# Mixer of a two-layer hybrid block: index keys first, index scores in two halves of the heads, four output tiles split among the last heads

## The chip, the cores and the metric

The kernel runs on one core of a Trainium2 chip. The metric is the device time of one execution in microseconds (us); the number quoted for the kernel before is the median of three runs. The engines are called TensorE (PE), VectorE (DVE), ScalarE (ACT), GpSimd (POOL) and SyncE (SP), as in the profile.

## The reference, cut to what matters

The program computes two hybrid layers (each: a feed-forward block, a mixer, a second feed-forward block), a norm, and then a second block of four other branches with a feed-forward block of its own. Everything is in 32-bit floats, for one sequence of 512 tokens of width 1024. The change lies in the mixer of the hybrid layers, which runs twice, once in each layer:

```python
h = rmsnorm(x, mix_norm) @ w_in
(a_q, a_k, a_v, b_q, b_k, b_v, i_q, i_k, i_w, c_q, c_kv, c_kr) = split_columns(h)
o_a = chunk_relpos_attention(a_q, a_k, a_v, a_rel_bias)          # 6 heads, additive relative bias
o_b = dsa_attention(rope(b_q), rope(b_k), b_v,                   # 5 heads, only the best 128 keys of a query
                    rope(i_q), rope(i_k), i_w)                   # 8 index heads of 32 choose them
o_c = mla_attention(c_q, c_kv, c_kr, ...)                        # 5 heads from two latents
x = x + jnp.concatenate([o_a, o_b, o_c], axis=-1) @ w_out
```

Inside `dsa_attention` the index heads give one score for each query and key, the sum over the eight heads of a weight times `relu(q_idx . k_idx)`; keys of later chunks get a large negative number, and the best 128 of each query are kept:

```python
dots = jnp.einsum('bqhd,bsd->bqhs', qi, k_idx) * (IDX_DIM ** -0.5)
score = jnp.einsum('bqh,bqhs->bqs', wi, jax.nn.relu(dots))
score = jnp.where(adm[None], score, NEG)
_, idx = lax.top_k(score, topk)
```

## The kernel before

Activations lie with features on the 128 partitions and the 512 tokens along the free axis. A matrix product in 32-bit precision is made of three TensorE passes over operands that are split into a high and a low part: `mm3` (L311 to L315) issues them, so that L313, L314 and L315 are the three passes of every such product. The split of an activation is one copy on ACT (L307) and one subtraction on DVE (L308, `split`); a weight is loaded on SP (L294), its high part is copied on ACT or POOL (L298) and its low part is a subtraction on DVE or POOL (L301).

The mixer is the method `mix(l)` from L593. It first projects the index queries (two tiles, `qi`) and then the tile that holds the index keys, the index weights and the rotary key of the C heads (tile 2: L619 to L634, with two small SP transfers at L620 and L621 and the split `ki` at the end). A rotary tile (`rope`, L561) scales the projection on DVE (L565), moves blocks of partitions with SP transfers into a tile `g`, multiplies on POOL (L570, L571) and adds on DVE (L572). The step `scores(i)` (L638) makes, for one block i of 128 queries, eight small products of index queries and keys, one for each index head, a ReLU on ACT (L648) and an accumulation on DVE (L650, L652), and then overwrites the inadmissible corner (`memset`). The generator `topk` (L655) then finds the best keys in 16 rounds for each of three blocks, each round a maximum of eight (L660) and a replacement (L661) on DVE; `some(n)` runs n of those 48 rounds.

The remaining steps are latents (L), values (V), the dense projections of A, B and C heads (a, b, c) and the heads themselves (A, B, C). A head computes logits on TensorE (L461 for A and B heads, `mm3` for C heads), adds the bias and takes the row maximum on DVE (L478), exponentiates on ACT (L483), inverts the sum on DVE (L484), scales on POOL (L485), transposes on TensorE (L517), copies and splits the transposed weights on ACT and DVE (L307, L308, tiles `pt`), multiplies with the values on TensorE (L526) and writes the output with a DVE addition (L535) into a tile of the `ys` slots. An A head first loads its bias with SP (L719) and POOL overwrites a corner of it (L720).

The string `MIX_PLAN` gives the order in which the program calls these steps. After the plan, all eight output tiles are split into `hs` slots (L771 to L777), and the output projection runs over them in the order 0, 1, 2, 6, 7, 3, 4, 5: for the first three of its eight column tiles seven of the eight inputs come first (`part`), so that they can be issued ahead of the last heads' end.

The instructions of each engine are not issued in the plan's order but in one that the framework's tile scheduler makes at build time from the plan and its own estimates. A shift in the plan can therefore move instructions of all engines in the whole mixer. Each engine takes its own list strictly in order: an instruction that waits holds back all that stand behind it on that engine.

```python
MIX_PLAN = ("S1 S2 S3 V0 a0 A0 A1 L0 a1 A2 L1 a2 V2 A3 t14 A4 A5 t4 c0 C0 c1 c2 t14 c3 V1 C1 C2 b0 t6 C3 t10 c4 t2 C4 t48 "
            "B0 B1 b1 B2 B3 b2 B4")
```

Of the kernel before, what the change touches and what calls it, by code (L numbers as in the profile page):

```python
# [10 lines left out]
def _warn_once_fixed(msg, *args, **kwargs):  # L11
# [12 lines left out]
S = 512  # L24
D = 1024
KD = 8
# [2 lines left out]
HALVES = ((0, 12), (12, 22))  # L29
DEPTH = 2  # L30
WENG = ("av", "ap")
MIX_PLAN = ("S1 S2 S3 V0 a0 A0 A1 L0 a1 A2 L1 a2 V2 A3 t14 A4 A5 t4 c0 C0 c1 c2 t14 c3 V1 C1 C2 b0 t6 C3 t10 c4 t2 C4 t48 "
            "B0 B1 b1 B2 B3 b2 B4")
FOX_PLAN = ("F0 Q0 K0 V0 Q1 H0 K1 H1 Q2 H2 K2 H3 V1 Q3 H4 K3 H5 Q4 H6 K4 H7 V2 Q5 H8 K5 H9 G0 Q6 H10 K6 G1 H11 V3 Q7 "
            "H12 G2 K7 H13 G3 H14 G4 H15 G5")
SB_PLAN = ("Q0 K0 V0 Q1 K1 H0 G0 H1 Q2 K2 H2 G1 H3 V1 Q3 K3 H4 H5 Q4 K4 H6 G2 H7 V2 Q5 K5 H8 H9 Q6 K6 H10 G3 H11 V3 Q7 K7 "
# [1 line left out]
NEG = -1e30  # L38
# [3 lines left out]
YAT = ((0, 0), (0, 1), (1, 0), (3, 0), (3, 1), (1, 1), (2, 0), (2, 1))  # L42
# [155 lines left out]
class Build:  # L198
# [394 lines left out]
    def mix(self, l):  # L593
        nc, I = self.nc, self.I
        hs, rb, rc = self.norm(f"mix_{l}", spill=True)
        ci, si, tk = (self.table(k) for k in (2, 3, 4))
        win = I[f"win_{l}"]

        def tile_of(n):
            w = self.weights(win[n], D)  # L600
            ps = self.ps()
            self.proj(ps, w, hs)
            return ps

        yslots = {}
# [7 lines left out]
            return yslots[a][64 * s:64 * s + 64, b, :]  # L613


        qi = [self.rope(tile_of(n), rb, 1.0, (ci, si), 16, tag="pt") for n in range(2)]
        ps = tile_of(2)
        f, g, kr = self.f(), self.f("g"), self.mx()
        nc.vector.tensor_mul(f, ps, rb)  # L619
# [8 lines left out]
        nc.tensor.matmul(pk, self.cst[:64, P:2 * P], f[:64], start=True, stop=True)  # L628
        ki = self.hl("pt")
        self.split(ki, pk)  # L630
        nc.gpsimd.tensor_mul(g[96:128], g[96:128], tk[96:128])
        nc.scalar.activation(g[64:96], g[96:128], AF.Copy)
        nc.gpsimd.tensor_add(kr[64:96], f[64:96], g[64:96])
# [1 line left out]

        sel = [None] + [self.mx() for _ in range(3)]

        def scores(i):  # L638
            n = (i + 1) * P
            t = slice(i * P, (i + 1) * P)  # L640
            sc = sel[i][:, :n]
            for h in range(8):
                r = slice(32 * (h % 4), 32 * (h % 4) + 32)
                q = qi[h // 4]
                ps = self.logits()
                self.mm3(ps[:, :n], q[r, 0, t], q[r, 1, t], ki[r, 0, :n], ki[r, 1, :n], True, True)
                e = self.f("fa")
                nc.scalar.activation(e[:, :n], ps[:, :n], AF.Relu)  # L648
                if h:
                    nc.vector.scalar_tensor_tensor(sc, e[:, :n], iw[:, 8 * i + h:8 * i + h + 1], sc, op0=OP.mult, op1=OP.add)  # L650
                else:
                    nc.vector.tensor_scalar(sc, e[:, :n], iw[:, 8 * i + h:8 * i + h + 1], None, op0=OP.mult)  # L652
            nc.vector.memset(sc[0:64, n - 64:n], NEG)

        def topk():  # L655
            for i in range(1, 4):
# [107 lines left out]
        def head_b(h):  # L764
            p, s = divmod(h, 2)
            self.head(*qk["b", p], None,
                      lambda i: sel[i][:, :(i + 1) * P] if i else self.chm[:, S - P:], vb[p], s, yout(6 + h))

        steps = {"S": scores, "L": lambda n: (latent_q, latent_kv)[n](), "V": lambda n: (values_a, values_b, values_c)[n](),
                 "a": dense_a, "A": head_a, "b": dense_b, "B": head_b, "c": dense_c, "C": head_c, "t": some}  # L770
        self.run(MIX_PLAN, steps)  # L771

        ys = [self.hl("hs") for _ in range(KD)]
        order = (0, 1, 2, 6, 7, 3, 4, 5)
        for k in order:
            a, b = YAT[k]
            self.split(ys[k], yslots[a][:, b, :])  # L777
        po = {}
        w = {}

# [566 lines left out]
```

## Time and profile before

| | us |
|---|---|
| median of three runs (lowest, highest) | 3539.57 (3539.09, 3543.49) |
| the profiled execution, its own time | 3545.66 |
| its span in the trace | 3543.9 |
| TensorE busy in the span | 3449.9 (97%) |
| VectorE busy | 1985.0 (56%) |
| GpSimd busy | 1485.8 (42%) |
| ScalarE busy | 1434.4 (40%) |

The first mixer lies at about 380 to 664 us of the span and the second at about 1420 to 1700 us; both run the same list of instructions with other buffers. The granted clock is TensorE's, as a share of its full 2.4 GHz; its other level is 1.2 GHz. A matmul's duration in the trace overlaps the next one's start, so what counts in a row of matmuls is the distance from start to start.

### The profile page before, as it was taken

The page shows a single profiled execution, that of the slowest core. Times are in us where ns is not written, and L with a number is a line of the kernel's source. Part 1 is how long each engine was busy: PE and PEld are TensorE (multiplying, and loading weights), DVE is VectorE, ACT ScalarE, POOL GpSimd, SP SyncE. Part 2 cuts the span into 40 slices and gives each one's busy share as a digit, 9 for nine tenths or more (in the row PEclk, how much of TensorE's full clock was granted, in tenths as well). Part 3 has the DMA queues.
Part 4 walks back from the last instruction along what each step waited for, and adds up shares of the span by engine and source line. Part 5 has one row for each costly group of instructions (what it writes and reads, how often), then busy time and mean ns, then how long its engine had stood idle before and what let it go on. Part 6 is the DMA issues. An engine that isn't in the chain of part 4 may idle for free.

```text
span 3543.9 us, 44752 instructions
## 1 busy us (share of the span) xinstructions
PE 3449.9 (97%) x16392; PEld 2866.2 (81%) x16392; DVE 1985.0 (56%) x3274; ACT 1434.4 (40%) x2366; POOL 1485.8 (42%) x1098
## 2 busy tenths in 40 slices
PE   8999999999999999999999999999999999999999
PEld 7888777788888888777888887888877788888887
DVE  5434697653445345796643456347636657757363
ACT  4223455532233223455422245346635545533222
POOL 3333346342424242446333443248645655435342
PEclk9999999999999999999999999999999999999999
DMA  3333433322333334334323233245532454442332
GB/s 134 91 105 107 130 94 108 114 98 92 101 94 101 90 101 129 104 96 118 113 94 109 84 125 113 96 129 143 154 123 93 147 178 128 128 143 95 96 101 90
DMA packets 141259, 397.57 MB, mean 112 GB/s; under 512 B 18144, under 2 KB 21600, under 8 KB 141040
## 3 DMA queue, kind: packets, MB, share of 16 engines
q1 hardware_dynamic: 141040, 394.71, 36.2%
q8 instruction: 130, 2.13, 0.2%
q14 instruction: 89, 0.73, 0.1%
HBM read 327.24 MB, written 20.48 MB: 98 GB/s over the span
## 4 chain that ended last, share of the span: by engine, by line
PE 48%; DVE 5%; ACT 2%; issue 1%; DMA 1%; POOL 1%; SPq 1%; DVEq 0%; ACTq 0%; POOLq 0%
PE pd L313 10%; PE pd L315 10%; PE pd L314 10%; PE pa L313 4%; PE pa L314 4%; PE pa L315 4%; PE po L526 1%; PE pt L517 1%; DVE wl L301 1%; PE pa L461 1%; ACT wh L298 1%; DVE st L1086 0%; DVE st L478 0%; SPq L454 0%; ACT st L483 0%
## 5 line engine op out<-in xcount | busy, mean ns | idle before, releaser
L301 POOL TENSOR_TENSOR wl<-raw,wh 128x1024 fp32r<-128x1024 f32 (+3 forms) x315 | 717.0, 2276 | 1158.2 <-ACT wh L298 1149.3
L298 ACT ACTIVATE wh<-raw 128x1024 fp32r<-128x1024 f32 (+3 forms) x631 | 609.6, 967 | 1336.6 <-PE pd L314 851.0
L313 PE MATMUL pd<-hs,wh 128*128 128x512 f32 (+1 forms) x2008 | 794.1, 396 | 21.0 <-ACT wh L298 7.7
L315 PE MATMUL pd<-hs,wl 128*128 128x512 f32 (+1 forms) x2008 | 792.7, 395 | 2.9 <-DVE wl L301 1.7
L314 PE MATMUL pd<-hs,wh 128*128 128x512 f32 (+1 forms) x2008 | 791.3, 394 | 1.1 <-DVE hs L308 1.0
L301 DVE TENSOR_TENSOR wl<-raw,wh 128x1024 fp32r<-128x1024 f32 (+3 forms) x316 | 384.0, 1215 | 230.6 <-ACT wh L298 224.0
L313 PEld LDWEIGHTS pd<-hs,wh 128*128 128x128 f32 (+1 forms) x2008 | 379.0, 189 | 102.6 <-ACT wh L298 14.0
L315 PEld LDWEIGHTS pd<-hs,wl 128*128 128x128 f32 (+1 forms) x2008 | 379.2, 189 | 86.6 <-DVE wl L301 4.6
L314 PEld LDWEIGHTS pd<-hs,wh 128*128 128x128 f32 (+1 forms) x2008 | 379.8, 189 | 81.7 <-DVE hs L308 2.7
L313 PE MATMUL pa<-hs,wh 128*128 128x512 f32 x896 | 349.6, 390 | 0.0
L314 PE MATMUL pa<-hs,wh 128*128 128x512 f32 x896 | 349.2, 390 | 0.0
L315 PE MATMUL pa<-hs,wl 128*128 128x512 f32 x896 | 349.2, 390 | 0.0
L413 POOL TENSOR_TENSOR f<-f,g 128x512 f32<-128x512 f32 x88 | 145.8, 1659 | 280.2 <-ACT g L411 273.8
L412 DVE TENSOR_TENSOR f<-pa,rb 128x512 f32<-128x512 f32 x88 | 60.8, 690 | 272.4 <-PE pa L315 272.4
L314 PEld LDWEIGHTS pa<-hs,wh 128*128 128x128 f32 x896 | 168.4, 188 | 35.0
L313 PEld LDWEIGHTS pa<-hs,wh 128*128 128x128 f32 x896 | 168.4, 188 | 34.7
L315 PEld LDWEIGHTS pa<-hs,wl 128*128 128x128 f32 x896 | 168.2, 188 | 34.9
L485 POOL TENSOR_SCALAR st<-st,ta 128x128 f32<-128x128 f32 x192 | 109.3, 573 | 94.2 <-DVE ta L484 81.7
L313 PE MATMUL pd<-ys,wh 128*128 128x512 f32 x362 | 143.9, 398 | 1.8 <-DVE f L740 1.7
L314 PE MATMUL pd<-ys,wh 128*128 128x512 f32 x362 | 142.6, 394 | 0.0
L315 PE MATMUL pd<-ys,wl 128*128 128x512 f32 x362 | 142.6, 394 | 0.0
L308 DVE TENSOR_TENSOR pt<-pt 128x384 fp32r<-128x384 f32 (+1 forms) x200 | 115.9, 595 | 32.7 <-ACT pt L307 31.7
(387 smaller groups left out, 6410.6 us busy)
## 6 DMA issues: line engine op xcount, KB each, us to landing
raw<-in_wg_dram SPq DMA_DIRECT2D x88, 512.0 KB, 3.4
raw<-in_wu_dram SPq DMA_DIRECT2D x88, 512.0 KB, 3.4
raw<-in_win_dram SPq DMA_DIRECT2D x38, 512.0 KB, 3.5
qk<-nt SPq DMA_DIRECT2D x76, 256.0 KB, 3.9
raw<-in_w2gt_dram SPq DMA_DIRECT2D x32, 512.0 KB, 3.4
raw<-in_w2br_dram SPq DMA_DIRECT2D x32, 512.0 KB, 3.3
qk<-nt SPq DMA_DIRECT2D x108, 128.0 KB, 2.5
raw<-in_wd1a_dram SPq DMA_DIRECT2D x32, 384.0 KB, 3.1
```

The lines of the kernel that those rows point to most:

```text
L298: nc.scalar.activation(h[:, :n], raw[:, :n], AF.Copy)
L301: (nc.vector if sub == "v" else nc.gpsimd).tensor_sub(lo[:, :n], raw[:, :n], h[:, :n].bitcast(FT))
L308: (eng or nc.vector).tensor_sub(dst[rows, 1, cols], src, dst[rows, 0, cols].bitcast(FT))
L313: mm(out, wh, xh, start=start, stop=False)
L314: mm(out, wh, xl, start=False, stop=False)
L315: mm(out, wl, xh, start=False, stop=stop)
L412: nc.vector.tensor_mul(u, pu, rb)
L413: nc.gpsimd.tensor_mul(ga, ga, s)
L461: self.nc.tensor.matmul(ps[:, :n], q[:, s, t], k[s][:, x, :n], start=x == 0, stop=x == 1)
L485: nc.gpsimd.tensor_scalar(st[:, c], st[:, c], sm, 0.0, op0=OP.mult, op1=OP.add)
L517: nc.tensor.transpose(pt[:, at + (i - j) * P:at + (i - j + 1) * P], st[:, OFF[i] + j * P:OFF[i] + (j + 1) * P], self.ident)
L526: nc.tensor.matmul(po[:, j * P:], va[:, o:o + P], w[:, x, c:c + S - j * P], start=j == 0 and x == 0, stop=j == 3 and x == 1)
```

## The change

Three edits of `mix`, in the order in which they stand. First, tile 2 (index keys, index weights, rotary key) is projected and treated ahead of the two `qi` tiles. Second, the scores are no longer made block by block with eight heads, but in two halves: `S0` makes heads 0 to 3 for all three blocks and `S1` heads 4 to 7, and only the second half overwrites the corner. The first half needs the first `qi` tile alone. Third, a new step Y splits output tiles 0, 1, 2 and 6 among the last B heads, into `ys` slots, which the latents have left by then; the other four are split after the plan, in `hs` slots, as before. The order of the output projection stays. No operation is added or taken away, and TensorE has 16392 matmuls in both.

```diff
-MIX_PLAN = ("S1 S2 S3 V0 a0 A0 A1 L0 a1 A2 L1 a2 V2 A3 t14 A4 A5 t4 c0 C0 c1 c2 t14 c3 V1 C1 C2 b0 t6 C3 t10 c4 t2 C4 t48 "
-            "B0 B1 b1 B2 B3 b2 B4")
+MIX_PLAN = ("S0 S1 V0 a0 A0 A1 L0 a1 A2 L1 a2 V2 A3 t14 A4 A5 t4 c0 C0 c1 c2 t14 c3 V1 C1 C2 b0 t6 C3 t10 c4 t2 C4 t48 "
+            "B0 Y0 B1 b1 Y1 B2 Y2 B3 b2 Y6 B4")
...
-        qi = [self.rope(tile_of(n), rb, 1.0, (ci, si), 16, tag="pt") for n in range(2)]
         ps = tile_of(2)
...
         self.split(ki, pk)
+        qi = [self.rope(tile_of(n), rb, 1.0, (ci, si), 16, tag="pt") for n in range(2)]
...
-        def scores(i):
+        def scores(a):
+            for i in range(1, 4):
+                four(i, a)
+
+        def four(i, a):
...
-            for h in range(8):
+            for h in range(4 * a, 4 * a + 4):
...
-            nc.vector.memset(sc[0:64, n - 64:n], NEG)
+            if a:
+                nc.vector.memset(sc[0:64, n - 64:n], NEG)
...
+        ys = {}
+
+        def early(k):
+
+            a, b = YAT[k]
+            ys[k] = self.hl("ys")
+            self.split(ys[k], yslots[a][:, b, :])
...
-        ys = [self.hl("hs") for _ in range(KD)]
         order = (0, 1, 2, 6, 7, 3, 4, 5)
         for k in order:
-            a, b = YAT[k]
-            self.split(ys[k], yslots[a][:, b, :])
+            if k not in ys:
+                a, b = YAT[k]
+                ys[k] = self.hl("hs")
+                self.split(ys[k], yslots[a][:, b, :])
```

Lines behind the edits move by 1 to 14 (L660 becomes L665, L661 becomes L666, L733 becomes L738). What the scheduler makes of it is seen in the lists of instructions.

The first place is on TensorE, in the first mixer, where the last C head ends and the B heads begin. Here pd_5457 is the last input projection of this stretch, pd_5611 and pd_5639 are the first two column tiles of the output projection with four inputs each (12 matmuls each), pm_5024 are the last logits of C4, pa_5070 and pa_5079 the first logits of B0. Before:

```order
L315 MATMUL pd_5457<-hs_2570,wl_5453 128x512
L313 MATMUL pd_5611<-hs_5581,wh_5606 128x512
...
L315 MATMUL pd_5611<-hs_5587,wl_5607 128x512
L313 MATMUL pm_5024<-qk_4961,qk_4988 128x512
...
L461 MATMUL pa_5070<-qk_4818,qk_4769 128x128 x2
L313 MATMUL pd_5639<-hs_5581,wh_5634 128x512
...
L315 MATMUL pd_5639<-hs_5587,wl_5635 128x512
L461 MATMUL pa_5079<-qk_4818,qk_4769 128x256 x2
```

Now (pd_5466 is the projection that was pd_5457, pa_5524 are the first logits of B4):

```order
L315 MATMUL pd_5466<-hs_2570,wl_5462 128x512
L313 MATMUL pm_5024<-qk_4961,qk_4988 128x512
...
L461 MATMUL pa_5070<-qk_4818,qk_4769 128x128 x2
L461 MATMUL pa_5079<-qk_4818,qk_4769 128x256 x2
...
L461 MATMUL pa_5524<-qk_5516,qk_5502 128x128 x2
L313 MATMUL pd_5611<-ys_5139,wh_5606 128x512
L313 MATMUL pd_5639<-ys_5139,wh_5634 128x512
```

The 24 matmuls of the output projection that stood around the first logits of B0 now stand some 45 rows later, behind the first logits of B4 and beside the products of B1 and B2.

The second place is on DVE at the same point of the program: hs_5581 to hs_5587 are the four split output tiles, st_4992 the softmax of C4, f_5290 a rotary tile of the B heads. Before:

```order
L308 TENSOR_TENSOR pt_4908<-pt_4904,pt_4908 128x384
L308 TENSOR_TENSOR hs_5581<-ys_3195,hs_5581 128x512
L308 TENSOR_TENSOR hs_5582<-ys_3195,hs_5582 128x512
L308 TENSOR_TENSOR hs_5583<-ys_3997,hs_5583 128x512
L308 TENSOR_TENSOR hs_5587<-ys_4570,hs_5587 128x512
L478 ISA st_4992,ta_4998<-pm_4994,chm_116 128x128
```

Now, at that place, and at the place to which the four have gone (pt_5194 and pt_5203 are transposed weights of B1):

```order
L308 TENSOR_TENSOR pt_4908<-pt_4904,pt_4908 128x384
L478 ISA st_4992,ta_4998<-pm_4994,chm_116 128x128
...
L308 TENSOR_TENSOR pt_5194<-pt_5190,pt_5194 128x384
L308 TENSOR_TENSOR ys_5139<-ys_3195,ys_5139 128x512
L308 TENSOR_TENSOR ys_5312<-ys_3195,ys_5312 128x512
L308 TENSOR_TENSOR ys_5386<-ys_3997,ys_5386 128x512
L308 TENSOR_TENSOR ys_5519<-ys_4570,ys_5519 128x512
L308 TENSOR_TENSOR pt_5203<-pt_5199,pt_5203 128x384
```

The four subtractions no longer stand ahead of C4's softmax; they stand among the softmaxes of B1 to B3.

The third place is on DVE in the middle of the first mixer, where head A3's softmax (st_3881) waits for its bias x_3878; x_2784 is the third block of the top-k. Before:

```order
L660 MAX t8_4924<-x_2784 128x8
L545 SCALAR_TENSOR_TENSOR e_3824<-pd_3826,rc_3719,e_3824 128x2x64
L545 SCALAR_TENSOR_TENSOR e_3824<-pd_3839,rc_3719,e_3824 128x2x64
L661 MATCH_REPLACE x_2784<-t8_4924,x_2784 128x512
L535 TENSOR_TENSOR ys_3195<-po_3566,fa_3633 64x512
L545 SCALAR_TENSOR_TENSOR e_3825<-pd_3826,rc_3719,e_3825 128x64
L545 SCALAR_TENSOR_TENSOR e_3825<-pd_3839,rc_3719,e_3825 128x64
L660 MAX t8_4927<-x_2784 128x8
L478 ISA st_3881,ta_3886<-pa_3883,x_3878 128x128
```

Now:

```order
L665 MAX t8_4840<-x_2784 128x8
L545 SCALAR_TENSOR_TENSOR e_3824<-pd_3839,rc_3719,e_3824 128x2x64
L666 MATCH_REPLACE x_2784<-t8_4840,x_2784 128x512
L545 SCALAR_TENSOR_TENSOR e_3825<-pd_3839,rc_3719,e_3825 128x64
L665 MAX t8_4918<-x_2784 128x8
L545 SCALAR_TENSOR_TENSOR v_3823<-pd_3852,rc_3719,v_3823 128x2x64
L478 ISA st_3881,ta_3886<-pa_3883,x_3878 128x128
```

The round that stands just ahead of st_3881 was the tenth of the third block (its second half, the replacement, follows behind); now it is the seventh, so three rounds more come behind that softmax. The lists of the second mixer move in the same way at the first two places.

## Rows read from the trace of the kernel before

**Rows 1.** Stages of the first mixer: window, length, busy us (instructions), granted clock, DMA

```profile
core 0: us, PE busy (x) PEld busy (x) DVE busy (x) ACT busy (x) POOL busy (x), PEclk, DMA share, GB/s
400.00:500.00 100.00, 100.00 (x489) 78.76 (x488) 91.34 (x234) 51.64 (x101) 44.02 (x39) 0.98 0.40 114
500.00:512.00 12.00, 8.71 (x44) 7.19 (x43) 10.02 (x30) 4.73 (x12) 2.29 (x3) 0.86 0.58 149
512.00:540.00 28.00, 23.41 (x102) 17.80 (x102) 27.03 (x73) 20.20 (x51) 15.61 (x19) 0.87 0.34 103
540.00:600.00 60.00, 59.44 (x336) 52.30 (x335) 39.77 (x102) 35.41 (x81) 34.66 (x34) 0.98 0.32 93
...
622.50:633.00 10.50, 7.04 (x43) 5.50 (x42) 6.95 (x23) 6.46 (x17) 7.69 (x10) 1.00 0.76 183
633.00:654.00 21.00, 19.79 (x110) 15.59 (x110) 16.66 (x56) 16.19 (x44) 9.53 (x17) 1.00 0.12 27
```

**Rows 2.** Waits of PE, 360 to 720 us: line, released by; us in total, times, longest

```profile
PE pa L461 <- DVE ta L478: 6.1, 7, 3.5
...
PE pd L313 <- DVE f L740: 1.7, 2, 1.4
```

**Rows 3.** PE timeline, start of the mixer: start, us, instruction [idle before, releaser]

```profile
387.55 0.50 PE L313 MATMUL pd<-hs,wh 128*128 128x512 f32 x1 [1.53 <-DVE f L565]
...
396.54 0.41 PE L624 MATMUL pa<-cst,f 8*128 8x8 f32 x4
```

**Rows 4.** Timelines of SP and DVE, the bias of head A3

```profile
502.92 3.06 SPq L454 DMA_DIRECT2D qk<-nt  x4
...
511.61 0.29 DVE L478 CUSTOM_DVE_ANT_0 st<-pa,x 128x128 f32<-128x128 f32 x1 [1.99 <-POOL x L720]
```

**Rows 5.** DVE groups by shape, 380 to 600 us: busy us, mean ns | idle before

```profile
L660 DVE MAX8 t<-x 128x8 f32<-128x512 f32 x16 | 10.8, 677 | 0.0
L661 DVE MATCH_REPLACE8 x<-t,x 128x512 f32<-128x512 f32 x16 | 10.8, 674 | 0.0
```

**Rows 6.** PE timeline, end of C4 and start of the B heads

```profile
608.90 0.39 PE L313 MATMUL pd<-hs,wh 128*128 128x512 f32 x1
609.13 0.39 PE L314 MATMUL pd<-hs,wh 128*128 128x512 f32 x1
...
612.38 0.39 PE L313 MATMUL pm<-qk 96*128 96x512 f32 x1
...
616.75 0.69 PE L461 MATMUL pa<-qk 128*128 128x128 f32 x2 [3.50 <-DVE ta L478]
618.17 0.77 PE L313 MATMUL pd<-hs,wh 128*128 128x512 f32 x1 [0.73 <-DVE f L565]
...
619.58 0.63 PE L313 MATMUL pd<-hs,wh 128*128 128x512 f32 x1
620.01 0.63 PE L314 MATMUL pd<-hs,wh 128*128 128x512 f32 x1
...
622.47 0.40 PE L461 MATMUL pa<-qk 128*128 128x256 f32 x2
```

**Rows 7.** DVE timeline, the same stretch

```profile
606.29 5.47 DVE L308 TENSOR_TENSOR hs<-ys,hs 128x512 fp32r<-128x512 f32 x4
...
612.94 2.82 DVE L572 TENSOR_TENSOR f<-f,g 128x512 f32<-128x512 f32 x1 [0.97 <-POOL g L571]
...
618.24 0.56 DVE L478 CUSTOM_DVE_ANT_0 st<-pa,chm 128x384 f32<-128x384 f32 x1
```

**Rows 8.** POOL timeline, the same stretch

```profile
609.60 1.60 POOL L570 TENSOR_TENSOR f<-f,x 128x512 f32<-128x512 f32 x1 [1.30 <-DMA g<-f]
...
612.87 2.34 POOL L301 TENSOR_TENSOR wl<-raw,wh 128x1024 fp32r<-128x1024 f32 x1
```

**Rows 9.** Durations, ns min/median/max: DVE splits of tile hs, 600 to 665 us; POOL L485, 600 to 664 us

```profile
L308 DVE TENSOR_TENSOR hs<-ys,hs x8: 679/692/2572, 606.3 to 661.8; 128x512 fp32r<-128x512 f32 x8
...
L485 POOL TENSOR_SCALAR st<-st,ta x24: 362/532/1213, 618.3 to 651.9; 128x128 f32<-128x128 f32 x6, 128x256 f32<-128x256 f32 x6, 128x384 f32<-128x384 f32 x6, 128x512 f32<-128x512 f32 x6
```

More of the change, by code (lines that the diff above doesn't have):

```diff
@@ L767, in head_b @@
                       lambda i: sel[i][:, :(i + 1) * P] if i else self.chm[:, S - P:], vb[p], s, yout(6 + h))
-        steps = {"S": scores, "L": lambda n: (latent_q, latent_kv)[n](), "V": lambda n: (values_a, values_b, values_c)[n](),
+        ys = {}
[3 more added lines that the diff above has]
+            self.split(ys[k], yslots[a][:, b, :])
+        steps = {"Y": early, "S": scores, "L": lambda n: (latent_q, latent_kv)[n](), "V": lambda n: (values_a, values_b, values_c)[n](),
                  "a": dense_a, "A": head_a, "b": dense_b, "B": head_b, "c": dense_c, "C": head_c, "t": some}
         self.run(MIX_PLAN, steps)
-        ys = [self.hl("hs") for _ in range(KD)]
         order = (0, 1, 2, 6, 7, 3, 4, 5)
         for k in order:
-            a, b = YAT[k]
-            self.split(ys[k], yslots[a][:, b, :])
+            if k not in ys:
+                a, b = YAT[k]
+                ys[k] = self.hl("hs")
+                self.split(ys[k], yslots[a][:, b, :])
         po = {}
```

## The prediction

> **What bounds the kernel now.** The busy shares come first: TensorE is busy 97% of the span, so what any edit of order can win is TensorE's idle time and its time at the lower clock, in the stretches that the edit touches. Next comes the view by stages of the first mixer [rows 1]. From 400 to 500 us TensorE has no idle time at all, with DVE busy 91.34 of 100. From 500 to 512 it is idle 12 - 8.71 = 3.29 us and from 512 to 540 us 28 - 23.41 = 4.59 us, at a granted clock of 0.86 and 0.87; DVE is busy 27.03 of the 28, so the latter stretch is DVE's. From 540 to 600 us TensorE is again full, with DVE at 39.77 of 60. Then come the B heads, where the idle time lies in single waits [rows 6]. The waits of TensorE over the mixer [rows 2] name DVE's softmax (6.1 us over seven waits, on L461 alone) before anything else. The second mixer runs the same list, so all terms are for one mixer and are doubled at the end.
>
> **Start: keys first.** Tile 2 moves ahead of the two query tiles. The wait of 1.53 us [rows 3] belongs to the row scale and stays: the third projection of the group waits for it, whichever tile that is. What is new is that the four small transposes of the index weights (0.41 us, [rows 3]) stand ahead of the third projection and wait for DVE's first product, which the projection needs anyway for its buffer. SP issues the two key transfers ahead of the sixteen of the query tiles instead of behind them. So the index scores can begin some microseconds earlier, and DVE begins its scores earlier too; TensorE has nothing to win from that up to 500 us, as it is never idle there. Price: between 0 and 0.8 us (the transposes, and as much waiting); I take **+0.4 us**, the row's own duration.
>
> **Middle: scores in halves, and where the top-k rounds land.** The head start is worth something only if DVE is further on at 512 us. Head A3's softmax stands in DVE's list behind a bias that SP fetches after the four stacking transfers of a key tile (502.92 us); DVE had run dry for 1.99 us when it came at 511.61 [rows 4]. The changed list leaves this chain as it is, so the 3.29 us from 500 to 512 us stay. And by that point in its list DVE has done three rounds fewer of the third block than before. A round costs 0.677 + 0.674 = 1.35 us [rows 5], so 3 x 1.35 = 4.05 us of DVE work move behind the bias, into the stretch in which DVE is the bound. In exchange, the products that release TensorE's projections (the key products of the C heads, L733 and L740) stand several microseconds of DVE work earlier. The waits for L740 make 1.7 us in two waits [rows 2]. Bounds: all 4.59 us of idle time go, or all 4.05 us of deferred rounds are waited for. I take **-1.7 us**, those two waits alone, because they are the ones whose releaser moves forward, while 20 us of free DVE time from 540 to 600 us [rows 1] can take the rounds.
>
> **End: four splits and 24 matmuls of the output projection move.** Before, the four splits take 5.47 us of DVE at 606.29 us, ahead of C4's softmax [rows 7], and the 24 matmuls that they release fill TensorE: twelve from 608.90 to 612.38 us, at a distance of 0.23 us, and twelve from 618.17 to 622.47 us, most of them 0.43 us apart, which is the 1.2 GHz level, after a wait of 3.50 us [rows 6]. In the changed list nothing stands between C4's last logits and B0's first two, and the 24 come behind B4's first logits.
>
> The wait for B0's first logits hardly moves. DVE's rotary addition at 612.94 us, which stands ahead of the softmax that releases them, waits for POOL, and POOL waited for a transfer until 609.60 us [rows 7, 8]; no split is in that chain. So TensorE now waits from about 609.6 us (608.90 and 0.7 us of logits) to about 616 us, where it waited 3.50 us before. B0's second logits then no longer stand behind twelve slow matmuls: they can start when the reduction of 618.24 us is through, at 618.80 [rows 7], instead of 622.47. That is a lead of 3.7 us for the whole chain of B heads. The 24 matmuls have to be paid later: 24 x 0.23 = 5.5 us, in the stretch that was 633 to 654 us, where TensorE had 21 - 19.79 = 1.2 us of idle time [rows 1]. Sum: 5.5 - 1.2 - 3.7 = **+0.6 us**. The lower bound: they also fill the 10.5 - 7.04 = 3.5 us of idle time from 622.5 to 633 us [rows 1], and DVE's addition shrinks from 2.82 us to a split's 0.69 [rows 7, 9], another 2.1: -5.0 us. The upper: they fill nothing, and the four splits, 4 x 0.69 = 2.8 us [rows 9], are waited for in the softmaxes of B1 to B3: 5.5 - 3.7 + 2.8 = +4.6 us. I take +0.6 because the new place lies in the fuller of the two stretches.
>
> DVE's addition of 2.82 us runs beside a GpSimd subtraction of 2.34 us that starts 0.07 us before it [rows 7, 8]. The Trainium skill ("SBUF — State Buffer", section "Who interferes with whom") says that a DVE instruction with two SBUF inputs and a GpSimd instruction that reads SBUF exclude each other for the whole of an instruction; this pair agrees with it (2.34 + 0.69 is near 2.82). By that rule each moved split could also wait for one of POOL's scalings (0.53 us in the middle, [rows 9]), and the upper bound would be an estimated 4 x 0.53 = 2.1 us higher, +6.7 us; the sum does not use it.
>
> **The sum.** +0.4 - 1.7 + 0.6 = -0.7 us for a mixer, -1.4 for both. The profiled execution of 3545.66 us (span 3543.9) would become 3544.3. It lies 6.1 us above the median of the runs, 3539.57; the difference carries over, so the forecast is **3538.2 us**. A measurement of this kernel can tell about 0.2% from no change, 7.1 us: I forecast no change that can be told.
>
> **Rivals.** *The heads keep their lead (faster).* The end comes at its lower bound because the late matmuls fall into the waits of B1 to B4: 0.4 - 1.7 - 5.0 = -6.3 us, -12.6 for both, 3527 us; with the whole idle time of 512 to 540 us gone as well, 0.4 - 4.6 - 5.0 = -9.2, 3521 us. For it: in that stretch all waits are for softmax and its followers, and DVE loses 5.47 us of work ahead of C4. Against it: the new place is full. Chance 0.31.
>
> *Deferred rounds on the critical engine (slower).* The heads' reductions and copies stand behind the three rounds, in a stretch in which DVE has 1 us free of 28. If TensorE waits for all of it: 0.4 + 4.05 + 0.6 = +5.1 us, +10.1 for both, 3549.7 us. It decides if the projections that now come earlier on TensorE are used up before DVE has caught up. For it: DVE's busy time; against it: its free time behind 540 us. Chance 0.13.
>
> *A start of the B heads without filler (slower).* After the 3.50 us wait TensorE ran most of twelve matmuls at the lower level [rows 6]. The wait will be some 6 us, and what follows are short matmuls with gaps. If they stay at 1.2 GHz, the 7.04 us of work from 622.5 to 633 us [rows 1] doubles, and the idle time there takes half of that: +3.5 us on top of an end at 5.5 - 3.7 = 1.8. So 0.4 - 1.7 + 1.8 + 3.5 = +4.0 us, +8.0 for both, 3547.6 us. It decides if the clock is still low when B0's third logits come. Chance 0.10. The Trainium skill ("TensorE: Matmul & The Clock Gate", section "Why this matters for your kernels") speaks for it: idle gaps between bursts of matmuls bring the clock back to half. The low row at 619.58 us agrees; what short matmuls with gaps do to it, no row here shows.
>
> *The lists move, the waits do not (no change).* The bias, the transfer to POOL and the row scale release what they released before, and the late matmuls fill exactly the lead: 3539.6 us. Chance 0.10.
>
> **How the numbers follow.** My forecast has 0.36 and the last rival 0.10: within 0.2%, 0.46. Faster 0.31; slower 0.13 + 0.10 = 0.23. The range 3524 to 3551 us holds the first case of the faster rival and both slower ones, and leaves out the deep end of the faster one and any sum of the slower two.
>
> **What would show it.** Right: DVE's first score some microseconds before 408 us; the wait for A3's bias of 2 us or more still there; the two L740 waits gone; one wait of about 6 us before B0's first logits; the 24 matmuls between 630 and 655 us at 0.23 us. Wrong: more idle time than 4.6 us behind the bias (the deferred rounds), a granted clock well under 1 in the ten microseconds behind B0's second logits (the lower level), or a B-head stretch that ends 3 us or more earlier (the lead kept).

## The result and the profile after

The changed kernel takes 3565.96 us (median of four runs, 3563.74 to 3569.25), the kernel before 3540.18 over the runs it is compared with: a ratio of 1.0067, with a 95% interval of 1.0055 to 1.0079. By that ratio it is 24 us slower, outside the range that was given, and slower where no change was forecast. The profiled execution took 3567.4 us, with a span of 3565.6.

The busy time first. TensorE has the same 16392 matmuls and is busy 10 us longer, in a span that is 22 us longer:

```profile
PE 3459.6 (97%) x16392; PEld 2871.4 (81%) x16392; DVE 1996.8 (56%) x3274; ACT 1435.0 (40%) x2366; POOL 1484.3 (42%) x1098
```

Then the stages of the first mixer in the changed kernel, the view of [rows 1]: window, length, busy time by engine, granted clock, DMA.

```profile
380.00:400.00 20.00, 18.47 (x84) 14.81 (x83) 7.35 (x15) 4.63 (x7) 9.15 (x6) 0.91 0.17 43
400.00:436.00 36.00, 36.00 (x174) 27.82 (x173) 20.93 (x35) 17.42 (x37) 13.96 (x10) 0.95 0.40 127
400.00:500.00 100.00, 98.36 (x473) 77.01 (x472) 84.27 (x203) 48.17 (x97) 38.87 (x33) 0.98 0.36 108
500.00:512.00 12.00, 10.35 (x58) 8.32 (x56) 11.93 (x32) 4.65 (x11) 4.63 (x5) 1.00 0.29 76
512.00:540.00 28.00, 22.05 (x85) 17.25 (x86) 25.40 (x71) 16.58 (x42) 10.08 (x16) 0.76 0.45 123
540.00:600.00 60.00, 55.56 (x319) 48.47 (x318) 46.80 (x124) 37.92 (x90) 31.20 (x33) 0.97 0.26 78
616.00:640.00 24.00, 15.22 (x70) 11.85 (x68) 16.24 (x44) 11.64 (x30) 19.77 (x20) 0.79 0.61 148
```

In the kernel before, three of these windows that [rows 1] does not have:

```profile
380.00:400.00 20.00, 18.47 (x98) 16.11 (x97) 5.74 (x14) 4.02 (x6) 7.25 (x5) 1.00 0.20 49
400.00:436.00 36.00, 36.00 (x175) 27.39 (x174) 29.40 (x64) 19.63 (x39) 18.03 (x11) 0.95 0.42 129
616.00:640.00 24.00, 18.80 (x94) 14.65 (x94) 17.13 (x59) 15.57 (x42) 16.39 (x21) 0.89 0.56 131
```

DVE does 20.93 us of work from 400 to 436 us where it did 29.40: a deficit of 8.5 us at the very place where the change was to give it a head start. It is made up from 540 to 600 us (46.80 against 39.77), and there TensorE, full before, is idle for 4.4 us (60 - 55.56). The waits of TensorE, the view of [rows 2], show the same: the softmax on DVE went from 6.1 to 10.3 us and the products of the C heads, which were to be released earlier, from 1.7 to 4.4 (L745 was L740).

```profile
PE pa L461 <- DVE ta L478: 10.3, 6, 5.3
PE pd L313 <- DVE f L745: 4.4, 2, 2.9
```

The work that comes late is the top-k. Here are its 48 rounds in the first mixer (shortest, median and longest duration of the maximum in ns, then first and last start in us), before and after:

```profile
L660 DVE MAX8 t<-x x48: 415/552/695, 417.4 to 535.3; 128x8 f32<-128x256 f32 x16, 128x8 f32<-128x384 f32 x16, 128x8 f32<-128x512 f32 x16
```

```profile
L665 DVE MAX8 t<-x x48: 407/554/697, 435.7 to 558.7; 128x8 f32<-128x256 f32 x16, 128x8 f32<-128x384 f32 x16, 128x8 f32<-128x512 f32 x16
```

The rounds of a block need the scores of all eight heads. Block by block, the first block had them at 417 us. In halves, every block is complete only in the second half, and the first round waits until 436 us, though DVE's first score came 1.9 us earlier than in the kernel before (406.73 against 408.65 us):

```profile
406.73 0.35 DVE L656 TENSOR_SCALAR x<-fa,iw 128x256 f32<-128x256 f32 x1
...
435.75 0.42 DVE L665 MAX8 t<-x 128x8 f32<-128x256 f32 x1
```

The bias of head A3, which the prediction took as fixed in time, comes 9 us later as well, by the same chain as in [rows 4]:

```profile
512.70 3.07 SPq L454 DMA_DIRECT2D qk<-nt  x4
...
520.36 0.29 DVE L478 CUSTOM_DVE_ANT_0 st<-pa,x 128x128 f32<-128x128 f32 x1 [1.93 <-POOL x L725]
```

**Where the 24 us lie.** A mixer's length can be read from the last transposes of the norm ahead of it (L355) to the first instruction of the norm behind it (L350); in kernels with the moved splits that L350 stands 1.3 us earlier in TensorE's list (the stretch from there to the next mixer is 1.3 us longer, 725.0 against 723.7), and 1.3 us are added. Idle time is TensorE's, length less busy time; the clock column is the sum of (1 - granted clock) x 5 us over windows of 5 us, so that a window at half speed counts half, whether TensorE was busy in it or not. Each row is one profiled execution, in us:

| kernel | mixer 1 | idle | clock | mixer 2 | idle | clock |
|---|---|---|---|---|---|---|
| before | 315.1 | 20.7 | 11.9 | 313.3 | 20.2 | 10.2 |
| changed | 328.5 | 27.7 | 18.7 | 324.1 | 26.8 | 13.6 |
| keys first | 316.0 | 19.5 | 11.9 | 314.7 | 19.8 | 10.2 |
| halves | 319.3 | 20.6 | 13.6 | 311.2 | 17.7 | 10.2 |
| moved splits | 317.6 | 22.1 | 13.7 | 318.5 | 26.0 | 10.2 |
| keys + halves | 325.2 | 27.5 | 11.9 | 318.8 | 23.8 | 10.2 |
| changed, first block whole | 320.1 | 22.5 | 10.2 | 322.4 | 23.8 | 15.4 |
| keys + halves, first block whole | 319.3 | 20.9 | 11.9 | 323.4 | 21.9 | 15.4 |

The change adds 13.4 and 10.8 us, together 24.2. The two profiled spans differ by less, 21.7 us, because the stretch behind the second mixer, which no edit touches, happened to be 2.6 us shorter; so the loss lies in the mixers. Of the 24.2 us, 13.6 are idle time: 7.7 of them from 60 to 215 us behind the norm, the middle, where the top-k and most of the A and C heads run, and 6.0 from 215 to 290 us, at the B heads (0.2 are saved at the start). With keys and halves and without the moved splits, all of the added idle time, 10.4 us, lies in the middle. The clock column grows by 10.2, but part of that falls on idle time and would count twice. Where TensorE was busy, the lower clock takes 25.3 us in the two mixers instead of 18.7, so 6.6 of the 24.2. The remaining 4 us count as busy time at full clock.

### The profile page after: what moved, and what is told of

Its sections match the earlier page's. It is cut to its first block, busy times and chain, and to the rows that moved or that the text cites. A ratio compares the mean times of both kernels' runs of the same rounds, so it can differ in the third digit from the quotient of the medians.

```text
span 3565.6 us, 44735 instructions
## 1 busy us (share of the span) xinstructions
PE 3459.6 (97%) x16392; PEld 2871.4 (81%) x16392; DVE 1996.8 (56%) x3274; ACT 1435.0 (40%) x2366; POOL 1484.3 (42%) x1098
## 4 chain that ended last, share of the span: by engine, by line
PE 82%; DVE 10%; ACT 3%; issue 2%; DMA 1%; SPq 1%; POOL 1%; DVEq 0%; ACTq 0%; POOLq 0%
PE pd L313 18%; PE pd L314 18%; PE pd L315 18%; PE pa L313 8%; PE pa L314 8%; PE pa L315 8%; PE po L526 2%; DVE wl L301 1%; DVE x L666 1%; PE pt L517 1%; DVE t L665 1%; PE pa L461 1%; DVE st L478 1%; ACT wh L298 1%; DVE pt L308 1%
## 5 line engine op out<-in xcount | busy, mean ns | idle before, releaser
L313 PE MATMUL pd<-hs,wh 128*128 128x512 f32 x1952 | 770.6, 395 | 17.1 <-ACT wh L298 7.9
L315 PE MATMUL pd<-hs,wl 128*128 128x512 f32 x1952 | 769.9, 395 | 2.7 <-DVE wl L301 2.0
L314 PE MATMUL pd<-hs,wh 128*128 128x512 f32 x1952 | 768.5, 394 | 0.2 <-DVE hs L375 0.2
L313 PEld LDWEIGHTS pd<-hs,wh 128*128 128x128 f32 x1952 | 367.8, 189 | 95.6 <-ACT wh L298 14.4
L315 PEld LDWEIGHTS pd<-hs,wl 128*128 128x128 f32 x1952 | 368.4, 189 | 83.6 <-DVE wl L301 5.4
L314 PEld LDWEIGHTS pd<-hs,wh 128*128 128x128 f32 x1952 | 368.6, 189 | 77.2 <-issue 2.0
L313 PE MATMUL pd<-ys,wh 128*128 128x512 f32 x418 | 166.0, 398 | 6.4 <-DVE f L745 5.7
L314 PE MATMUL pd<-ys,wh 128*128 128x512 f32 x418 | 164.7, 394 | 0.0
L315 PE MATMUL pd<-ys,wl 128*128 128x512 f32 x418 | 164.3, 393 | 0.0
L485 POOL TENSOR_SCALAR st<-st,ta 128x128 f32<-128x128 f32 x192 | 108.0, 566 | 132.7 <-DVE ta L484 106.9
```

The source lines that it names most:

```text
L313: mm(out, wh, xh, start=start, stop=False)
L314: mm(out, wh, xl, start=False, stop=False)
L315: mm(out, wl, xh, start=False, stop=stop)
L485: nc.gpsimd.tensor_scalar(st[:, c], st[:, c], sm, 0.0, op0=OP.mult, op1=OP.add)
```

## The experiments

Each ratio is against the kernel before on the same chip, with its 95% interval; differences in us are the ratio less 1, times 3540. The first three are one part of the change alone.

**Halves alone.**

```diff
-MIX_PLAN = ("S1 S2 S3 V0 a0
+MIX_PLAN = ("S0 S1 V0 a0
...
+        def scores(a):
+            for i in range(1, 4):
+                four(i, a)
```

> The kernel before with the scores in two halves alone. Theory 1 (the first top-k block is complete only when the second half is done, the rounds start some 18 us later, and DVE, which bounds the middle, lacks that work early): 3555 to 3575 us, first top-k maximum of the first mixer 15 us or more behind 417 us, DVE busy under 25 of the 36 us from 400 to 436. Theory 2 (the moved splits leave the B heads' start without filler): 3540 us, within 5.

Measured 1.001 (1.000 to 1.0019): +3.5 us. Its first round starts as late as in the changed kernel, and DVE is busy 24.9 of the 36 us from 400 to 436. So the mark of theory 1 is there and its price is not: it was a miss.

```profile
400.00:436.00 36.00, 36.00 (x186) 27.48 (x185) 24.91 (x37) 19.89 (x40) 19.35 (x13) 1.00 0.44 145
...
436.48 0.43 DVE L665 MAX8 t<-x 128x8 f32<-128x256 f32 x1
```

**Moved splits alone.**

```diff
-            "B0 B1 b1 B2 B3 b2 B4")
+            "B0 Y0 B1 b1 Y1 B2 Y2 B3 b2 Y6 B4")
```

> The kernel before with the four splits among the last B heads alone. Theory 1: 3536 to 3545 us, the top-k as before. Theory 2: 3550 to 3565 us, with a wait of 5 us before the first logits of the B heads and the lower clock behind it.

Measured 1.0027 (1.0017 to 1.0036): +9.6 us, just under the lower edge of what theory 2 expected, with the long wait that it named. B0's first logits start at 615.60 us after a wait of 5.44 us, and the second ones at 617.72, where they started at 622.47 [rows 6]:

```profile
615.60 0.69 PE L461 MATMUL pa<-qk 128*128 128x128 f32 x2 [5.44 <-DVE ta L478]
617.72 0.79 PE L461 MATMUL pa<-qk 128*128 128x256 f32 x2 [1.43 <-DVE ta L478]
```

**Keys first alone.**

```diff
-        qi = [self.rope(tile_of(n), rb, 1.0, (ci, si), 16, tag="pt") for n in range(2)]
         ps = tile_of(2)
...
         self.split(ki, pk)
+        qi = [self.rope(tile_of(n), rb, 1.0, (ci, si), 16, tag="pt") for n in range(2)]
```

> The kernel before with the index keys projected first alone. Theory 1: the rounds start some 2 us earlier, so 3534 to 3541 us. A third theory (the keys' place itself costs: its transfers and GpSimd work ahead of the rotary tiles): 3545 us or more.

Measured 1.001 (1.000 to 1.0019): +3.5 us, between the two theories. The first round starts at 419.3 us, 2 us later, not earlier.

**Changed kernel without the halves** (scores block by block, the rest as changed):

> The changed kernel with the scores block by block again (keys first and the moved splits stay). Theory 1: 3532 to 3545 us, nearly all of the loss gone. Theory 2: 3555 us or more, the loss stays.

Measured 1.0032 (1.0020 to 1.0044): +11.3 us. Between both expectations: undoing the halves takes some 12 of the 24 us away.

**Changed kernel without the moved splits** (keys first and halves):

> Keys first and halves, the splits behind the plan as before. The halves alone cost 4 us, the keys alone 4. If they only add: 3546 to 3551 us. If both delay the same thing, DVE's work ahead of the middle, and DVE's lag counts only beyond some slack: 3553 to 3562 us, with C4's last logits 5 us or more later than in the kernel before.

Measured 1.0054 (1.0039 to 1.0069): +19 us, where the two parts alone have 3.5 each, as the second case expected. These two edits hurt together: 12 us of the 24 come only when both are in. With both, C0's last logits start at 557.9 us in the first mixer, against 551.7 with the halves alone, 548.2 with the keys alone and 545.3 before: 12.6 us late, where the parts alone make 6.4 and 2.9.

**Changed kernel with the keys in their old place** (halves and moved splits):

> Halves and moved splits, the keys in their old place. If the parts add: 4 + 9 = 13, 3551 to 3556 us. If the halves cost more whenever the out-projection's matmuls are not there to fill the B heads' start: 3560 us or more.

Measured 1.0029 (1.0020 to 1.0038): +10 us. That is within its interval (7 to 13.5 us) both the 13 us of the first case, in which the parts add, and the 9.6 of the moved splits alone. Taken out one at a time, the keys first carry 14 of the 24 us, the halves 12 and the moved splits 5.

**First block whole, then halves.** The changed kernel with its first block's eight heads first:

```diff
-            for i in range(1, 4):
+            if a == 0:
+                four(1, 0)
+                four(1, 1)
+            for i in range(2, 4):
                 four(i, a)
```

> The changed kernel, but the first block of scores is made whole (both halves) before the halves of the other two blocks, so that the top-k rounds can begin. If the late first block is what the halves cost: 3547 to 3555 us, about that of the kernel with the scores block by block, and the first maximum before 425 us. If the order of the other blocks matters as much: 3559 us or more.

Measured 1.0040 (1.0026 to 1.0055): +14 us, between the two cases. It takes 10 of the 24 us away, and its first round is at 417.5 us. **The same without the moved splits:**

> Keys first, the first block of scores whole and the halves for the other two, moved splits undone (all rounds whole). With all halves it was 19 us slower. By the late first block: 3543 to 3549 us. By the order of the lists: 3555 us or more.

Measured 1.0042 (1.0028 to 1.0056): +15 us. That is a miss for the late first block, and within 0.2 us of the 3555 us that the order of the lists would give (the median is 3554.83 us). The 19 us with all halves (1.0039 to 1.0069) cannot be told from it. The rounds run from 417.9 to 529.4 us, no later than in the kernel before:

```profile
L668 DVE MAX8 t<-x x48: 412/553/696, 417.9 to 529.4; 128x8 f32<-128x256 f32 x16, 128x8 f32<-128x384 f32 x16, 128x8 f32<-128x512 f32 x16
```

Its first mixer is 4.2 us and its second 10.1 us longer than before, with only 0.1 and 1.7 us more idle time; in the second 5.2 us more go to the clock. What is left, about 4 and 3 us, is neither; it counts as TensorE's busy time at full clock. So the whole first block does what it was meant to do, with the idle time: 10.4 us more than before fall to 1.8, and with the moved splits 13.6 fall to 5.4. But with keys and halves most of the time does not go with it, so the late first round is not all that is wrong there.

**Half of the top-k left out**, in the kernel before and in two others. It was meant to tell whether DVE's rounds carry the loss.

```diff
-                    nc.vector.max(m8, sc)
-                    nc.vector.match_replace(sc, m8, sc, -3e38)
+                    part = sc[:, :64 * (i + 1)]
+                    nc.vector.max(m8, part)
+                    nc.vector.match_replace(part, m8, part, -3e38)
```

The kernel before: 

> Leaves out half of the top-k: each of the 48 rounds looks at the first half of the columns only (DVE work of the rounds about halved, number and order of the rounds kept). The kernel before, so the base of the next two. If DVE's rounds bound the middle: 3525 to 3536 us. If they do not: 3538 to 3544.

Keys and halves: 

> Keys first and halves, moved splits undone, and half of the top-k left out as in the run before it. With whole rounds these two edits cost 19 us. If they cost by DVE's rounds starting late and DVE lagging: 0 to 7 us over before_th. If the new order of the lists costs by itself (TensorE's and SP's places): 14 us or more over before_th.

All three edits: 

> All three edits, half of the top-k left out. With whole rounds 24 us. By DVE's lag: only what the moved splits cost remains, 6 to 12 us over before_th. By the lists' order: 18 us or more over before_th.

Measured 3525.25 us (ratio 0.9957, 0.9942 to 0.9972), 3530.67 (0.9970, 0.9958 to 0.9981) and 3537.59 (0.9992, 0.9982 to 1.0001). With half of the rounds' work, keys and halves cost 5.4 us instead of 19, and all three edits 12.3 instead of 24. The middle, 500 to 545 us, in keys and halves with whole rounds and then with half of them:

```profile
500.00:545.00 45.00, 32.78 (x150) 25.38 (x150) 42.24 (x109) 24.21 (x58) 19.65 (x24) 0.92 0.43 117
```

```profile
500.00:545.00 45.00, 40.28 (x217) 34.00 (x216) 37.89 (x113) 30.74 (x76) 25.13 (x30) 0.96 0.47 135
```

TensorE is idle 12.2 us in the one and 4.7 us in the other, and the number of rounds is the same. Most of the loss goes with the length of the rounds, as it would if it needed a full DVE. But the runs differ in more than that: for shorter rounds the scheduler writes other lists. Of DVE's 583 instructions in the first mixer, 455 stand in the same order (the longest that both lists share) in keys and halves with whole and with half of the rounds; the kernel before and keys and halves share 453. So a loss by the order of the lists is not ruled out. The kernel before gains 15 us by the same edit, which fits a middle that is DVE's, with the same reserve: the two lists share 482.

**Where the moved splits stand.** Three more places for the four splits, on the kernel before. All ahead of the first B head:

```diff
-            "B0 B1 b1 B2 B3 b2 B4")
+            "Y0 Y1 Y2 Y6 B0 B1 b1 B2 B3 b2 B4")
```

> The kernel before with the four splits in the latents' slots, but all of them ahead of the first B head in the plan, so that the out-projection's matmuls stand ahead of B0's logits again. If the missing filler made the 9 us of the moved splits: 3536 to 3544 us. If the slots made them (the latents' slots instead of hs, and what is freed when): 3547 us or more.

Two ahead and two behind ("Y0 Y1 B0 Y2 B1 b1 Y6 B2 B3 b2 B4"): 

> The kernel before with the moved splits in two portions: tiles 0 and 1 ahead of the first B head, 2 and 6 behind it, so that twelve of the 24 matmuls stand ahead of B0's first logits again and the rest later. Before this run: all late cost 9 us, all early cost 10. If the spread of the filler over the B heads' start makes the cost: 3540 to 3547 us. If it is the latents' slots or the changed lists elsewhere: 3548 us or more.

All ahead of the last B head ("B0 B1 b1 B2 B3 b2 Y0 Y1 Y2 Y6 B4"): 

> The kernel before with all four moved splits just ahead of the last B head, so that no matmul of the output projection can fill before B4. If missing filler at the B heads' start is the cost: 3552 us or more, with more idle time there than in the kernel with the splits among the heads. If the splits' place on DVE among B1 to B3 is the cost: 3540 to 3547 us.

Measured 1.0028 (1.0019 to 1.0037), 1.0022 (1.0012 to 1.0032) and 1.0027 (1.0016 to 1.0037): +10, +8 and +9.5 us. Early, late or spread, it makes no difference that can be told. With all four ahead, the 24 matmuls stand ahead of B0's first logits again and the wait there is back to 3.26 us, and the cost stays:

```profile
619.68 1.14 PE L461 MATMUL pa<-qk 128*128 128x128 f32 x4 [3.26 <-DVE ta L478]
```

So neither the filler's place nor the splits' place on DVE is the cause by itself, and theory 2 falls in that form. What the four traces have in common is idle time at the B heads, 215 to 290 us behind the norm: 11.9 to 12.2 us in the first mixer and 13.1 to 13.6 in the second, against 10.8 and 10.0 before. That is 4 to 5 us of the 8 to 10.

**The bias on another queue.** The A heads' bias is loaded from ScalarE's queue, on the kernel before:

```diff
-            nc.sync.dma_start(bt, I[f"rel_{l}"][h])
+            nc.scalar.dma_start(bt, I[f"rel_{l}"][h])
```

> The kernel before with the A heads' bias loaded by ScalarE's queue, so that it does not stand behind the stacking transfers on SP. The prediction took that wait for a bound of the middle. If it is: DVE's wait of 2 us for A3's bias goes and the middle shortens by 2 to 6 us in each mixer, 3528 to 3537 us. If DVE's backlog bounds the middle anyway: 3538 to 3543 us.

Measured 0.9996 (0.9987 to 1.0005): no change that can be told. The transfer is issued 2 us earlier, at 503.99 us, and the softmax that needs it starts only 0.7 us earlier, after a longer wait:

```profile
501.87 3.11 SPq L454 DMA_DIRECT2D qk<-nt  x4
...
503.99 0.33 ACTq L719 DMA_DIRECT2D x<-in_rel_dram  x1
...
510.72 0.14 POOL L720 MEMSET x<- 64x64 f32 x1 [8.88 <-DMA x<-in_rel_dram]
...
510.90 0.29 DVE L478 CUSTOM_DVE_ANT_0 st<-pa,x 128x128 f32<-128x128 f32 x1 [3.12 <-POOL x L720]
```

In the kernel before, the bias was issued at 506.02 us:

```profile
506.02 2.27 SPq L719 DMA_DIRECT2D x<-in_rel_dram  x2
...
511.17 0.14 POOL L720 MEMSET x<- 64x64 f32 x1 [8.28 <-DMA x<-in_rel_dram]
```

POOL's overwrite, which waits for the landing, comes 0.45 us earlier, and the stacking transfers themselves stand 1.05 us earlier in this execution (501.87 against 502.92 us [rows 4]). So beside them the bias gained nothing: its place behind them on SP is not what it waits for alone. No run that does the whole top-k was faster than the kernel before by more than its interval.

## Why the prediction was wrong, step by step

**The start (+0.4 us)** was small when alone, as forecast, though above its bounds of 0 to 0.8: keys first alone lengthened the two mixers by 0.9 and 1.4 us, in all of their stretches together. Beside the halves it was not small (19 us together against 3.5), and the prediction has no term for that. What it said of DVE was wrong, too. The prediction let DVE "begin its scores earlier too", and took that for a head start at 512 us. The scores did begin 1.9 us earlier; DVE's work as a whole came later, because 48 rounds hang on complete scores, not on first ones. By 500 us DVE had done 7.1 us less work from 400 us on than before (84.27 against 91.34).

**The middle (-1.7 us)** is the step that failed: it was to win 3.4 us in the two mixers, and TensorE's idle time there grew by 7.7. "DVE has done three rounds fewer" was read from the order at one instruction and priced at 4.05 us, as if that instruction came at the same time. It came 9 us later (520.36 against 511.61 us), and the last round 23 us later (558.7 against 535.3). "The changed list leaves this chain as it is" held for the order of the chain and not for its time, and the 3.29 us of idle time from 500 to 512 us did not stay: 1.65 are left there, and the wait has moved behind 512 us. The 1.7 us that were to be won at L740 (the product of a C head's queries, not of its keys, as the prediction has it) became 4.4 us of waiting, and the free DVE time behind 540 us did take the rounds, but not without TensorE waiting 4.4 us there. The rival of the deferred rounds came nearest, "if the projections that now come earlier on TensorE are used up before DVE has caught up", with too small a size: its cap was the three rounds. Its sign, more than 4.6 us of idle time behind the bias, came, but by little: 5.3 us in the 28 us behind it.

```profile
520.36:548.36 28.00, 22.72 (x89) 17.59 (x90) 27.29 (x71) 18.34 (x44) 15.82 (x19) 0.80 0.33 99
```

How much of this is shown? That the late first block makes idle time beside the keys first: with the first block whole 8 to 9 us of it go, in both pairs of kernels (each read from one execution, and with other lists, as after every edit). Not shown is that it makes the loss by itself. With the halves alone the rounds are as late (the last one at 564.9 us) and the cost is 3.5 us; with keys, halves and the first block whole the rounds are in time and 15 us remain. That the loss needs a full DVE fits the runs with half of the top-k, in which 14 of 19 us go, but their lists differ as well. With keys and halves together C0's logits are later than the two delays added; which places in the lists do that is left open, and with it the cause of the 12 us that only both edits together make.

**The end (+0.6 us)** had its parts right. The wait before B0's first logits was put at about 6 us and is 5.44 with the splits alone (5.25 in the changed kernel); the lead of B0's second logits was put at 3.7 us and is 4.75. The 24 matmuls come later, as said; in the changed kernel from 650 to 657 us, most of them at 0.23 us. The sum was still wrong: the moved splits alone make the mixers 2.5 and 5.2 us longer. In the first mixer 1.8 us of that are the clock, the third rival's mechanism: from 616 to 640 us it is 0.81, where it was 0.89 with two portions of matmuls around B0.

```profile
616.00:640.00 24.00, 18.57 (x86) 14.02 (x86) 19.14 (x65) 17.05 (x47) 17.81 (x23) 0.81 0.48 111
```

The sign that the prediction named for it came in the changed kernel: in the ten microseconds behind B0's second logits the clock is 0.66, where it was 1.00 before.

```profile
627.78:637.78 10.00, 8.42 (x32) 6.65 (x33) 7.56 (x25) 6.25 (x18) 8.26 (x10) 0.66 0.76 180
```

```profile
622.47:632.47 10.00, 6.95 (x42) 5.41 (x40) 6.95 (x23) 6.31 (x16) 7.19 (x9) 1.00 0.80 193
```

In the second mixer of the moved splits alone it is 5.8 us of idle time. 2.7 of them lie 115 to 160 us behind the norm (10.7 against 8.0 us), ahead of every edited step: the scheduler's lists differ there too, and a wait for L740 of 2.8 us appears that the kernel before does not have. In the first mixer the lists are the same up to there, and so is the idle time (7.8 and 7.9 us). What makes the idle time at the B heads for all four places of the splits stays open; the slots themselves were not tried apart from the order.

**The clock** had no term in the sum. 6.6 of the 24.2 us are busy time lost to the lower clock, which the prediction named in one rival only, for one place. **The sum of parts** was also wrong in kind: the three parts alone give 3.5 + 3.5 + 9.6 = 16.6 us, the whole 24. The plainest sign is keys and halves, 7 us as a sum and 19 (14 to 24) measured.

## What to carry to other kernels

When an order of loops is turned, look for the first result that is complete, not for the first that is begun: here the consumer of whole blocks (48 rounds on the engine that bounds the middle) lost 18 us of start while the producer won 2. What that costs is another question: 3.5 us alone, far more beside a second edit. So price edits together, and not one by one. Where an instruction's place in a list is compared between two kernels, its time must be followed too; a chain that keeps its order can still move as a whole. And where a scheduler writes the lists, a small edit can be paid in stretches that it does not touch, in idle time and in time at the lower clock.

## What the runs showed of the hardware

The same wait of 1.53 us at the mixer's start, with the same busy time behind it, was followed by a granted clock of 1.00 in the kernel before and of 0.91 in the changed one (380 to 400 us, the first rows of both groups above). That is 0.09 of 20 us, 1.8 us, in the one and nothing in the other. The clock also falls without a wait: from 400 to 436 us TensorE is busy all 36 us in the kernel before, in the changed one and with the halves alone, and the clock is 0.95, 0.95 and 1.00. The Trainium skill ("TensorE: Matmul & The Clock Gate", section "What's actually happening") says that a monitor of the array's activity sets the clock to one of two levels. No run here shows what the monitor counts; these windows show only that equal idle time need not give an equal clock.

A small transfer did not come sooner here by leaving a busy queue. Issued 2 us earlier on ScalarE's queue, beside the four stacking transfers on SP, which stood 1.05 us earlier themselves, the bias landed 0.45 us and was used 0.7 us earlier. The Trainium skill ("DMA: Bandwidth & Descriptors", section "Issuing engines are not separate DMA queues") says that transfers of all issuing engines run on the same DMA engines, and this pair agrees with it.
